# Branches around an expert's third token tile: behind every second weight tile instead of every fourth

## The chip, the cores and the metric

The kernel runs on one core of a Trainium2 chip. Its metric is the device time of one launch in microseconds (us). TensorE (PE in the profile; its weight loads are PEld) multiplies matrices, VectorE (DVE), ScalarE (ACT) and GpSimd (POOL) work on elements, and SyncE (SP) starts the transfers of weights from HBM into SBUF. Every engine runs its own list of instructions, and semaphores order them among each other.

## The reference

The reference is a decoder trunk of two layers over 256 tokens of width 1024. Each layer has a token mixer (three kinds of attention heads that share one projection) and a channel mixer, a SwiGLU: a dense one of width 2816 in layer 0, and in layer 1 a mixture of eight experts of width 3584. Only the experts matter here:

```python
def _swiglu(h, w_gate, w_up, w_down):
    return (jax.nn.silu(h @ w_gate) * (h @ w_up)) @ w_down

def _moe(h, router_w, w_gate, w_up, w_down):
    ...
    logits = (t @ router_w).astype(jnp.float32)
    top_val, top_idx = lax.top_k(logits, TOP_K)          # TOP_K = 2 of 8
    top_w = jax.nn.softmax(top_val, axis=-1)
    ...
    for e in range(N_EXPERTS):
        y = y + combine[:, e:e + 1] * _swiglu(t, w_gate[e], w_up[e], w_down[e])
```

Each token goes to two of eight experts, so an expert has 64 tokens on average. All weights are float32; the eight experts hold 8 x 3 x 1024 x 3584 x 4 bytes = 352 MB, which are read once.

## The kernel before

The kernel gathers an expert's tokens into at most 96 columns (`xg`, by a matmul with a one-hot matrix at line 1252), as three *token tiles* of 32. The weights are the moving side of the matmuls and the tokens the stationary side: four matmuls with 32 columns each stand beside each other on the array, one for each quarter of a weight tile's columns.

An expert's width of 3584 is cut into two halves of 2048 and 1536 (`WS`). For each half `moe_pass` runs `project` with the gate weights (PSUM `mm`), SiLU on ACT into `a`, `project` with the up weights (PSUM `up`), the product `a*up` on DVE (line 1337), and nine or twelve transposes (`turn_units`, line 1221) into `aT`. `back` multiplies `aT` with the down weights into `y`; it runs one half late, behind the next half's projections. When both halves are in `y`, `take` and `scatter` weight the result and add it to `X`.

A *weight tile* is one transfer of up to 1 MB into one of 14 buffers (`raw`): for gate and up one of eight blocks of 128 rows, for down two blocks of 128 rows. So a gate or up piece has eight weight tiles, the down piece of the first half eight and that of the second half six. SP starts the transfers in program order; each waits for its buffer to come free and for the transfer eight places earlier.

Expert 0 always runs all three token tiles. The other seven are sorted by load, and their counts stand in registers (`many`). For these, `project` and `back` run token tiles 0 and 1 plainly, and keep the third tile's matmuls for a branch: `third` emits an `If(many > 64)` whose body runs the third tile over the weight tiles collected so far. The first branch of a piece that starts a PSUM bank also has an else side that writes zeros (`zerb`, lines 1140 and 1141), since the bank would otherwise hold nothing. Where there is none, the else side holds one semaphore step that stands for the skipped matmuls. A scheduler decides where the two plain token tiles stand among the branches. Two conditions place the branches: line 1161 for gate and up, line 1186 for down.

Of the kernel before, what the change touches and what calls it, by code (L numbers as in the profile page):

```python
# [31 lines left out]
def kernel(  # L32
# [1087 lines left out]
    def pieces(src, r, n):  # L1120

        step = 2048 // n
        for i in range(0, r, step):
            m = min(step, r - i)
            yield i, m, load_w(src[:, i:i + m], m, n)

    def place(banks, t, w):

        per = 512 // w
        return banks[t // per], t % per * w  # L1130

    def third(many, run, b, o, n=None):

        with tc.If(many > 64) as more:
            run()
        if n != 0:
            with more.Else():
                for c in range(0, n, 256):
                    m = min(256, n - c)
                    pe.matmul(b[:, o + c:o + c + m], zerb, trib.rearrange("p a n -> p (a n)")[:, 0:m], start=(o + c == 0), stop=True,  # L1140
                              skip_group_check=True)

    def project(x, n, src, w, banks, many):

        nw = w // 4

        def tile_t(t, k, v):
            b, o = place(banks, t, nw)
            xs = x[:, k, C * n + 32 * t:C * n + 32 * t + 32]
            for j in range(4):  # L1150
                last_of = pe.matmul(b[32 * j:32 * j + 32, o:o + nw], xs, v[:, nw * j:nw * j + nw],  # L1151
                                    start=(k == 0 and o == 0), stop=(k == KD - 1), skip_group_check=True)
            return last_of.ins

        rows, z = [], nw
        for k0, m, raw in pieces(src, KD, w):
            for k in range(m):
                rows.append((k0 + k, raw[:, k]))
                for t in range(2 if many is not None else T3):
                    marks["x"] = tile_t(t, k0 + k, raw[:, k])  # L1160
            if many is not None and (k0 + m) % 4 == 0:
                third(many, lambda: [tile_t(2, k, v) for k, v in rows], *place(banks, 2, nw), n=z)
                rows, z = [], 0

    def back(aT, w, src, banks, first, last, many):

        nw = w // 4
        R = w // P

        def tile_t(t, m, v):  # L1170
            j, cc = m * P // nw, m * P % nw // P
            b, o = place(banks, t, 256)
            for q in range(4):
                last_of = pe.matmul(b[32 * q:32 * q + 32, o:o + 256], aT[:, cc, t, 32 * j:32 * j + 32], v[:, 256 * q:256 * q + 256],  # L1174
                                    start=(first and m == 0 and o == 0), stop=(last and m == R - 1), skip_group_check=True)
            return last_of.ins

        rows, z, tiles = [], 256 if first else 0, 0
        for ms, raw in down_tiles(src, w):
            for i, m in enumerate(ms):  # L1180
                v = raw[:, D * i:D * i + D]
                rows.append((m, v))
                for t in range(2 if many is not None else T3):
                    marks["y"] = tile_t(t, m, v)
            tiles += 1
            if many is not None and (tiles == 4 or ms[-1] == R - 1):
                third(many, lambda: [tile_t(2, m, v) for m, v in rows], *place(banks, 2, 256), n=z)
                rows, z, tiles = [], 0, 0

    def down_tiles(src, w):  # L1190


        if w // 4 % 256 == 0:
            v = src.rearrange("(g p i) n -> p g (i n)", p=P, i=2)
            for g in range(w // 256):
                yield [2 * g, 2 * g + 1], load_w(v[:, g:g + 1], 1, 2 * D)[:, 0]
        else:
            v = src.rearrange("(g p i) n -> p g (i n)", p=P, i=3)
            one = src.rearrange("(g p i) n -> p g i n", p=P, i=3)
            for g in range(w // 384):  # L1200
                yield [3 * g, 3 * g + 1], load_w(v[:, g:g + 1, 0:2 * D], 1, 2 * D)[:, 0]
                if g % 2:
                    yield [3 * g - 1, 3 * g + 2], load_w(one[:, g - 1:g + 1, 2], 2, D).rearrange("p a n -> p (a n)")
# [21 lines left out]
    def moe_pass(base):  # L1225
# [74 lines left out]
        def finish(p):  # L1300
            nonlocal ybanks
            e, aT, w, src, first, last = p
            if first:
                ybanks = [dn2_bank() for _ in range(2)]
            back(aT, w, src, ybanks, first, last, None if base or e == 0 else many[e])
            if last:
                late.append((e, turn_hot(e), *take(ybanks)))

        for e in range(NE):
# [12 lines left out]
            for s_, w in enumerate(WS):  # L1322
                nw = w // 4
                gs = groups(nw)
                gb = [mm_bank() for _ in gs]
                project(xg, (e + 1) % 2, wg[:, :, c0:c0 + w], w, gb, None if base or e == 0 else many[e])
                a = fpm.tile([P, T3, 512], F32, tag="a", name="a", bufs=1)
                for b, t0, n in gs:
                    act.activation(a[:, t0:t0 + n, 0:nw], gb[b][:, 0:n * nw].rearrange("p (t n) -> p t n", t=n), AF.Silu)  # L1329
                if late:  # L1330
                    with tc.issue_after(marks["x"]):
                        scatter(*late.pop())
                ub = [up_bank() for _ in gs]
                project(xg, (e + 1) % 2, wu[:, :, c0:c0 + w], w, ub, None if base or e == 0 else many[e])
                for b, t0, n in gs:
                    av = a[:, t0:t0 + n, 0:nw]
# [29 lines left out]
    many = [None]  # L1366
# [94 lines left out]
```

## Time and profile before

| what | us |
|---|---|
| three timed runs | 1403.47, 1404.56, 1405.38 (median 1404.56) |
| profiled execution | 1399.66 |
| its span, first to last instruction | 1397.8 |
| PE busy | 1328.8 (95%) |
| DVE, ACT, POOL busy | 515.0, 366.1, 226.9 |
| expert stage, from about 540 us on: weight stream | about 420 GB/s in most slices |

The span has two parts: attention and the dense layer up to about 540 us, and the experts after it. In the second part the transfer engines move about 420 GB/s nearly all the time, and PE is busy 9 tenths or more of nearly every slice. The page counts a matmul as busy until its modelled end; matmuls overlap, so that a run's busy time is a little longer than the distance to the next run's start. Each float32 matmul of the program stands twice in the trace.

### The profile page before, as it was taken

Reading aid. Unit: us, or ns where it says so; the run is one execution under the profiler, and the core shown is the slowest. Engines: PE = TensorE matmul, PEld = TensorE weight load, DVE = VectorE, ACT = ScalarE, POOL = GpSimd, SP = SyncE. Lnnn points to the kernel's source line nnn. Section 1 sums busy time; section 2 is a strip of 40 time slices with the busy share of each in tenths; the row PEclk is TensorE's granted clock in tenths of the full one; section 3 lists DMA queues with packets and bytes.
Section 4 is the critical chain, followed back from the end, with each engine's and each line's share of the span. In section 5 each row is a group of like instructions: output and inputs, shape, how many; then the busy total and the mean of one; then the engine's idle time right before and its main releaser. Section 6 shows DMA issues by size and latency. Waiting matters only on the chain. (4 is left out here: it accounts for less than half of the span.)

```text
span 1397.8 us, 29383 instructions
## 1 busy us (share of the span) xinstructions
PE 1328.8 (95%) x12537; PEld 770.6 (55%) x12537; DVE 515.0 (37%) x778; ACT 366.1 (26%) x750; POOL 226.9 (16%) x257
## 2 busy tenths in 40 slices
PE   7999989999999999999999999998999999999995
PEld 3767768889777774354553343452442453454542
DVE  5788687788895653000110200200200200210213
ACT  4476544444466741000100100100100100100102
POOL 3334345444552341000000000000000000000000
PEclk9999999999999999999999999999999999999997
DMA  9866567988773368999999999999999999999992
GB/s 356 338 225 214 207 229 267 325 295 308 264 266 111 118 249 298 297 423 416 403 422 421 419 422 422 418 422 421 420 422 422 416 423 422 382 420 408 418 420 94
DMA packets 104678, 476.85 MB, mean 341 GB/s; under 512 B 8220, under 2 KB 17060, under 8 KB 75854
## 3 DMA queue, kind: packets, MB, share of 16 engines
q1 hardware_dynamic: 104278, 473.77, 86.4%
q8 instruction: 116, 1.90, 0.5%
q10 hardware_dynamic: 152, 0.80, 0.1%
q14 instruction: 36, 0.29, 0.1%
q0 software_dynamic: 96, 0.08, 0.0%
HBM read 472.78 MB, written 1.84 MB: 340 GB/s over the span
## 5 line engine op out<-in xcount | busy, mean ns | idle before, releaser
L1174 PE MATMUL y<-raw,aT 128*32 128x256 f32 x4480 | 258.2, 380 | 12.5 <-DMA raw<-in_moe_w_down_dram 5.5
L1151 PE MATMUL up<-raw,xg 128*32 128x512 f32 (+1 forms) x2560 | 255.5, 540 | 3.8 <-DMA raw<-in_moe_w_up_dram 2.8
L1151 PE MATMUL mm<-raw,xg 128*32 128x512 f32 (+1 forms) x2560 | 250.9, 540 | 4.9 <-DMA raw<-in_moe_w_gate_dram 2.5
L1174 PEld LDWEIGHTS y<-raw,aT 128*32 128x32 f32 x4480 | 157.3, 110 | 110.0 <-issue 17.0
L1151 PEld LDWEIGHTS up<-raw,xg 128*32 128x32 f32 x2560 | 82.4, 110 | 160.8 <-issue 150.5
L136 POOL TENSOR_TENSOR lo<-raw,hi 128x192 fp32r<-128x192 f32 x126 | 145.7, 1161 | 150.9 <-ACT hi L130 140.2
L1151 PEld LDWEIGHTS mm<-raw,xg 128*32 128x32 f32 x2560 | 81.9, 110 | 158.5 <-issue 138.7
L1337 DVE TENSOR_TENSOR a<-a,up 128x512 f32<-128x512 f32 (+1 forms) x48 | 29.8, 621 | 364.2 <-PE up L1151 226.2
L134 DVE TENSOR_TENSOR lo<-raw,hi 128x832 fp32r<-128x832 f32 (+2 forms) x126 | 136.4, 1090 | 41.8 <-ACT hi L130 37.0
L130 ACT CAST hi<-raw 128x1024 fp32r<-128x1024 f32 (+2 forms) x126 | 124.8, 1001 | 102.7 <-PE mm L153 43.8
L1377 POOL TENSOR_SCALAR ss_f<-ss_f 128x1 f32<-128x1 f32 x2 | 0.4, 218 | 856.9 <-ACT up L1375 856.9
L152 PE MATMUL mm<-hi,xT_hi 128*128 128x512 f32 (+2 forms) x336 | 131.8, 395 | 0.0
L153 PE MATMUL mm<-hi,xT_lo 128*128 128x512 f32 (+2 forms) x336 | 130.8, 389 | 0.5 <-DVE xT_lo L366 0.5
L154 PE MATMUL mm<-lo,xT_hi 128*128 128x512 f32 (+2 forms) x336 | 129.8, 388 | 1.3 <-DVE lo L134 1.3
L282 DVE SCALAR_TENSOR_TENSOR acc<-raw,c_act,acc 128x1024 f32<-128x1024 f32 x80 | 108.6, 1357 | 6.0 <-DMA raw<-in_w_ada_dram 5.5
L1329 ACT ACTIVATE a<-mm 128x512 f32<-128x512 f32 (+1 forms) x48 | 26.1, 544 | 212.6 <-PE mm L1151 148.8
L1222 ACT COPY aT<-tp 128x512 f32<-128x512 f32 (+1 forms) x32 | 16.0, 506 | 248.4 <-PE tp L1221 248.2
L154 PEld LDWEIGHTS mm<-lo,xT_hi 128*128 128x128 f32 x336 | 64.6, 192 | 12.9 <-DVE lo L134 2.8
L1222 DVE COPY aT<-tp 128x512 f32<-128x512 f32 x16 | 11.1, 692 | 164.1 <-PE tp L1221 164.0
L152 PEld LDWEIGHTS mm<-hi,xT_hi 128*128 128x128 f32 x336 | 64.8, 193 | 11.7 <-ACT a L836 1.4
L153 PEld LDWEIGHTS mm<-hi,xT_lo 128*128 128x128 f32 x336 | 64.8, 193 | 11.4 <-DVE xT_lo L366 1.3
L1267 ACT COPY Y<-y 32x256 f32<-32x256 f32 x48 | 17.5, 366 | 198.5 <-DVE Y L1265 198.0
(363 smaller groups left out, 1344.3 us busy)
## 6 DMA issues: line engine op xcount, KB each, us to landing
raw<-in_moe_w_down_dram SPq DMA_DIRECT2D x112, 1024.0 KB
raw<-in_moe_w_gate_dram SPq DMA_DIRECT2D x64, 1024.0 KB
raw<-in_moe_w_up_dram SPq DMA_DIRECT2D x64, 1024.0 KB
raw<-in_moe_w_gate_dram SPq DMA_DIRECT2D x64, 768.0 KB
raw<-in_moe_w_up_dram SPq DMA_DIRECT2D x64, 768.0 KB
raw<-in_w_ada_dram SPq DMA_DIRECT2D x40, 1024.0 KB
raw<-in_w_in_dram SPq DMA_DIRECT2D x12, 1024.0 KB
raw<-in_ffn_w_down_dram SPq DMA_DIRECT2D x10, 1024.0 KB
```

The lines of the kernel that those rows point to most:

```text
L130: act.copy(hv, raw)
L134: marks["lo"] = dve.tensor_sub(lo[:, :n1], f[:, :n1], hi[:, :n1]).ins
L136: pool.tensor_sub(lo[:, n1:a * n], f[:, n1:], hi[:, n1:a * n])
L152: pe.matmul(ps, xh, wh, start=start, stop=False)
L153: pe.matmul(ps, xl, wh, start=False, stop=False)
L154: pe.matmul(ps, xh, wl, start=False, stop=stop)
L282: dve.scalar_tensor_tensor(acc, raw[:, j], ck, acc, op0=OP.mult, op1=OP.add)
L1151: last_of = pe.matmul(b[32 * j:32 * j + 32, o:o + nw], xs, v[:, nw * j:nw * j + nw], start=(k == 0 and o == 0), stop=(k == KD - 1), skip_g ...
L1174: last_of = pe.matmul(b[32 * q:32 * q + 32, o:o + 256], aT[:, cc, t, 32 * j:32 * j + 32], v[:, 256 * q:256 * q + 256], start=(first and m ...
L1222: (dve.tensor_copy if b0 == 4 else act.copy)(flat[:, b0 * P:(b0 + len(part)) * P], tb[:, :len(part) * P])
L1329: act.activation(a[:, t0:t0 + n, 0:nw], gb[b][:, 0:n * nw].rearrange("p (t n) -> p t n", t=n), AF.Silu)
L1337: dve.tensor_mul(av, av, ub[b][:, 0:n * nw].rearrange("p (t n) -> p t n", t=n))
```

## The change

Both conditions change: in `project` a branch is emitted behind every second weight tile, and in `back` too.

```diff
@@ project
-            if many is not None and (k0 + m) % 4 == 0:
+            if many is not None and (k0 + m) % 2 == 0:
                 third(many, lambda: [tile_t(2, k, v) for k, v in rows], *place(banks, 2, nw), n=z)
                 rows, z = [], 0
@@ back
-            if many is not None and (tiles == 4 or ms[-1] == R - 1):
+            if many is not None and (tiles == 2 or ms[-1] == R - 1):
                 third(many, lambda: [tile_t(2, m, v) for m, v in rows], *place(banks, 2, 256), n=z)
                 rows, z, tiles = [], 0, 0
```

On PE, in the first gate piece of the last expert, from its first matmul on. `mm` is the PSUM bank, `xg` the tokens, `raw` the weights; the rows at line 1151 between a COMPARE_AND_BRANCH and the next UNCONDITIONAL_BRANCH are the third token tile, the other rows at line 1151 tiles 0 and 1 (eight matmuls a weight tile). Before:

```order
L1151 MATMUL mm<-raw,xg 32x512 x24
L1134 COMPARE_AND_BRANCH
L1151 MATMUL mm<-raw,xg 32x512 x16
L1134 UNCONDITIONAL_BRANCH
L1140 LDWEIGHTS zerb
L1140 MATMUL mm<-trib,zerb 128x256
L1140 LDWEIGHTS zerb
L1140 MATMUL mm<-trib,zerb 128x256
L1134 UNCONDITIONAL_BRANCH
L1151 MATMUL mm<-raw,xg 32x512 x32
L1134 COMPARE_AND_BRANCH
L1151 MATMUL mm<-raw,xg 32x512 x16
```

The same piece now, from behind the zeros of its first branch to the bottom of the piece:

```order
L1151 MATMUL mm<-raw,xg 32x512 x16
L1134 COMPARE_AND_BRANCH
L1151 MATMUL mm<-raw,xg 32x512 x8
L1134 UNCONDITIONAL_BRANCH x2
L1151 MATMUL mm<-raw,xg 32x512 x16
L1134 COMPARE_AND_BRANCH
L1151 MATMUL mm<-raw,xg 32x512 x8
L1134 UNCONDITIONAL_BRANCH x2
L1151 MATMUL mm<-raw,xg 32x512 x16
L1134 COMPARE_AND_BRANCH
L1151 MATMUL mm<-raw,xg 32x512 x8
L1134 UNCONDITIONAL_BRANCH x2
```

One branch without zeros has become three, each over 8 matmuls instead of 16, and between two branches stand 16 plain matmuls instead of 32.

On PE, at the end of the last expert's last down piece (`y` is its PSUM, `aT` the turned products; 16 plain matmuls are one weight tile). Before:

```order
L1174 MATMUL y<-raw,aT 32x256 x32
L1134 COMPARE_AND_BRANCH
L1174 MATMUL y<-raw,aT 32x256 x32
L1134 UNCONDITIONAL_BRANCH x2
L1174 MATMUL y<-raw,aT 32x256 x32
L1134 COMPARE_AND_BRANCH
L1174 MATMUL y<-raw,aT 32x256 x16
L1134 UNCONDITIONAL_BRANCH x2
L1174 MATMUL y<-raw,aT 32x256 x16
```

Now:

```order
L1134 COMPARE_AND_BRANCH
L1174 MATMUL y<-raw,aT 32x256 x16
L1134 UNCONDITIONAL_BRANCH x2
L1174 MATMUL y<-raw,aT 32x256 x32
L1134 COMPARE_AND_BRANCH
L1174 MATMUL y<-raw,aT 32x256 x16
L1134 UNCONDITIONAL_BRANCH x2
L1174 MATMUL y<-raw,aT 32x256 x32
L1134 COMPARE_AND_BRANCH
L1174 MATMUL y<-raw,aT 32x256 x16
L1134 UNCONDITIONAL_BRANCH x2
L1174 MATMUL y<-raw,aT 32x256 x16
```

Two branches have become three; the longest skip, over 32 matmuls, is gone, and the last plain weight tile still stands behind the last branch.

## Rows read from the trace of the kernel before

**Rows 1.** The page's costliest groups: form and count | busy, mean ns | idle before.

```profile
L1174 PE MATMUL y<-raw,aT 128*32 128x256 f32 x4480 | 258.2, 380 | 12.5 <-DMA raw<-in_moe_w_down_dram 5.5
```

**Rows 2.** One line's instructions, line 1140: count, ns min/median/max, first and last start.

```profile
L1140 PE MATMUL y<-trib,zerb x4: 283/283/283, 720.0 to 1350.8; 128*128 128x256 bf16 x4
```

**Rows 3.** Timeline of PE, straight runs: start, us, form, count [idle before].

```profile
616.16 20.93 PE L1174 MATMUL y<-raw,aT 128*32 128x256 f32 x384
...
1175.01 20.81 PE L1151 MATMUL up<-raw,xg 128*32 128x512 f32 x192
1195.63 0.61 PE L1174 MATMUL y<-raw,aT 128*32 128x256 f32 x8
...
1250.87 20.95 PE L1174 MATMUL y<-raw,aT 128*32 128x256 f32 x384
```

**Rows 4.** Stages: window, length, busy PE, PEld, DVE, ACT, POOL; PEclk, DMA, GB/s.

```profile
937.00:1046.00 109.00, 102.33 (x1238) 45.18 (x1234) 14.26 (x24) 10.77 (x23) 0.00 (x0) 1.00 1.01 421
1046.00:1153.00 107.00, 106.05 (x1338) 46.41 (x1331) 11.75 (x20) 8.13 (x17) 0.00 (x0) 1.00 1.01 420
1153.00:1273.00 120.00, 119.90 (x1511) 56.24 (x1509) 13.18 (x24) 10.09 (x22) 0.00 (x0) 1.00 1.00 409
1273.00:1376.00 103.00, 99.50 (x1283) 47.65 (x1286) 13.95 (x24) 9.89 (x23) 0.00 (x0) 1.00 0.93 384
```

**Rows 5.** Waits of PE, 940 to 1046 us: us in total, times, longest.

```profile
PE y L1174 <- DMA raw<-in_moe_w_down_dram: 3.0, 4, 1.3
PE up L1151 <- DMA raw<-in_moe_w_up_dram: 2.4, 4, 1.0
```

**Rows 6.** Waits of PE, 1046 to 1376 us.

```profile
PE y L1174 <- issue: 1.9, 1, 1.9
...
PE mm L1151 <- DMA raw<-in_moe_w_gate_dram: 0.5, 1, 0.5
```

**Rows 7.** Stages, the end of the weight stream.

```profile
1370.00:1376.00 6.00, 5.65 (x104) 3.53 (x100) 0.83 (x2) 0.21 (x1) 0.00 (x0) 1.00 0.08 30
```

**Rows 8.** Timeline of PE in the last expert.

```profile
1293.84 7.07 PE L1151 MATMUL up<-raw,xg 128*32 128x512 f32 x64
1301.09 1.92 PE L1151 MATMUL up<-raw,xg 128*32 128x512 f32 x16 [0.18 <-PEq L1134]
...
1367.18 3.66 PE L1174 MATMUL y<-raw,aT 128*32 128x256 f32 x64
1371.02 3.66 PE L1174 MATMUL y<-raw,aT 128*32 128x256 f32 x64 [0.18 <-PEq L1134]
1374.85 1.93 PE L1174 MATMUL y<-raw,aT 128*32 128x256 f32 x32 [0.17 <-PEq L1134]
```

**Rows 9.** One line's instructions, the branch line 1134.

```profile
L1134 PEldq COMPARE_BRANCH  x120: 70/179/2089, 640.9 to 1373.2; - x120
L1134 PEldq EVENT_SEMAPHORE  x28: 51/51/51, 641.7 to 1374.7; - x28
```

**Rows 10.** Timeline of PE, its last waits for weights.

```profile
979.70 5.60 PE L1174 MATMUL y<-raw,aT 128*32 128x256 f32 x100 [0.49 <-DMA raw<-in_moe_w_down_dram]
...
1035.72 4.42 PE L1174 MATMUL y<-raw,aT 128*32 128x256 f32 x64 [1.29 <-DMA raw<-in_moe_w_down_dram]
...
1045.66 10.51 PE L1151 MATMUL mm<-raw,xg 128*32 128x512 f32 x96 [0.54 <-DMA raw<-in_moe_w_gate_dram]
```

**Rows 11.** Waits of SP's queue from 560 us on.

```profile
SPq L113 <- DMA raw<-in_moe_w_down_dram: 141.0, 73, 2.7
```

**Rows 12.** Timeline of PE, two long idle times at skips.

```profile
1094.06 1.93 PE L1174 MATMUL y<-raw,aT 128*32 128x256 f32 x32 [0.77 <-PEq L1134]
...
1359.05 0.59 PE L1174 MATMUL y<-raw,aT 128*32 128x256 f32 x3
1361.57 1.92 PE L1174 MATMUL y<-raw,aT 128*32 128x256 f32 x29 [1.93 <-issue]
```

## The prediction

> **What bounds the kernel now.** I read the table of stages first, then TensorE's waits on either side of one moment (1046 us), then the branch line itself, then single runs of matmuls.
>
> An expert with at most 64 tokens skips its third token tile; I call it light, the others heavy. Counting matmuls, 4480 at line 1174 [rows 1] are twice 2240 (the trace shows every fp32 matmul twice): expert 0 has 336, seven others 224 each, which leaves 336 for third tiles, at 112 each three experts. So three are heavy and four light, and four `zerb` matmuls on `y`, the last at 1350.8 us, say the same [rows 2]. That last one puts a light expert at the end. Of the order in time: a run of 192 up matmuls without a break [rows 3] marks a heavy expert, `zerb` matmuls a light one, and so the eight are: expert 0 (no branch), light, light, heavy, light, heavy, heavy, light.
>
> In the table of stages the reader is to see that both resources look full [rows 4]: weights at 409 to 421 GB/s and TensorE busy for 102.33 of 109 us before 1046 us, 119.90 of 120 in the second of the two neighbouring heavy experts. Busy shares can't choose between them; waits can. From 940 to 1046 us TensorE waits eight times for down and up weights (3.0 and 2.4 us) [rows 5]. From 1046 to 1376 us the only weight wait is the one with which that window opens, 0.5 us; the longest of the rest is "issue", 1.9 us, TensorE's own sequencer [rows 6]. So up to 1046 us the weight stream sets the time, and from there to 1376 us TensorE does, without slack, with one stretch of light work (the fifth expert's last down piece, at 1086 to 1096 us) and the last light expert inside. At the end the weights have run out (30 GB/s after 1370 us [rows 7]) while TensorE still works to 1376.8 us [rows 8].
>
> **The change part by part.** *More branches.* Per expert: 2 become 4 in two gate pieces, two up pieces and the first down piece, and 2 become 3 in the second down piece (six weight tiles): 12 to 23, 84 to 161 in all. Five of them also write zeros where the tile is skipped; those stay five. A light expert thus passes 18 plain skips instead of 7.
>
> *What a plain skip costs on TensorE.* The arm's else side is an EVENT_SEMAPHORE, 28 in the trace [rows 9], seven for each of four light experts. It waits for TensorE's own earlier matmuls, so the pipeline runs empty and fills again. Price: 64 up matmuls with one skip behind them take 1301.09 - 1293.84 = 7.25 us [rows 8]; 192 without a break take 1195.63 - 1175.01 = 20.62, so 64 take 6.87 [rows 3]. Difference 0.38. In the down piece 64 take 3.84 (1367.18 to 1371.02) and 3.83 us [rows 8] against 64/384 of 20.93 = 3.49 [rows 3]: 0.35. I take 0.37. Only half of it shows as idle time (0.18 [rows 8]); the other half is the overlap of neighbouring matmuls that is lost. The low end is therefore 0.18, the high end 0.38.
>
> The Trainium skill (Advanced Engine Details and Errata, Control Flow Timing) gives about 51 ns for a plain branch and about 108 ns for a compare-and-branch. The trace has 51 ns for the semaphore step, but 70 to 2089 ns for the compare. By the page's prices alone 12 skips would cost an estimated 1.9 us and the kernel would come out at 1406.5 us; the rows say 0.35 to 0.38 a skip, because the drain, not the instruction, is paid.
>
> *Where it counts.* After 1046 us: 11 more skips in the last expert, and one more in the fifth expert's last down piece. 12 x 0.37 = 4.4 us on the path, bounds 2.2 and 4.6. Queued behind a waiting semaphore step are the next weight tiles' matmuls, and for these wait ACT and DVE (`a`, `Y`) and, at the end, the whole tail; nothing absorbs the delay. The granted clock is 1.00 (the 2.4 GHz level) in light and heavy stretches alike [rows 4], so the clock stays out of the sum.
>
> *Skips before 1046 us.* 33 less that one, 32, cost 12 us of TensorE time, but the stream sets the time there. The tightest place is the fifth expert: between the waits that end at 979.70 and 1035.72 us six more skips (two gate, two up, two down) come to 2.2 us, against idle times of 1.29 and 0.54 us that they use up [rows 10]. 0.4 us is left. It is paid back right there: at 1045.66 us TensorE waits for the third weight tile of a heavy expert while third-token-tile work on the first two could run; behind four tiles it may not, behind two it may. I cost this at 0, bounds -0.5 and +0.4. If the cover were gone (a stream that runs earlier), up to 2.2 us would show.
>
> *Executed arms.* In the heavy experts the arm falls through. 384 down matmuls take 20.93 us in expert 0, which has no branch, and 20.95 in a heavy expert with two [rows 3]: 0.01 us a branch. 22 more after 1046 us cost 0.2 us. The cover is the queue of matmuls that TensorE's sequencer has issued ahead; without it, the compare (median 179 ns [rows 9]) would stand bare, 22 x 0.18 = 4.0 us. The number of matmuls is the same on both sides, so nothing else is added.
>
> *Weight buffers and other queues.* A buffer is free after two tiles' arm instead of four, so transfers may be issued earlier. After 1046 us TensorE waits for no transfer, so this buys nothing. SP passes 77 more block borders, but stands mostly in waits for earlier transfers (141.0 us for down weights alone [rows 11]); ACT and DVE are busy 10.09 and 13.18 us of 120 [rows 4]. All three at 0; if an SP issue came late it would have to be by more than the stream's lead to reach TensorE.
>
> **Sum**, on the profiled execution (1399.66 us, span 1397.8): 4.4 + 0.2 + 0 = 4.6 us, 1404.3 us. The timed runs of before have a median of 1404.56, 4.9 us above the profiled one; the difference is carried over: 1409.2 us. Own range of this case: 2.2 - 0.5 = 1.7 to 4.6 + 0.2 + 0.4 = 5.2 us more, 1406.3 to 1409.8 us; I stand near its top because the skips measured at 0.35 to 0.38 are the nearest rows.
>
> **Rivals.** (1) *Skips that wait for code.* One compare took 2089 ns [rows 9] (the idle time at 1094.06 us is 0.77 instead of 0.18, 0.6 more), and 0.2 us after a skip, inside a plain run of matmuls, TensorE stood 1.93 us for nothing that the profile shows [rows 12]: 2.5 us over the 14 skips after 1046 us, those with zeros included, 0.18 for each. If each taken branch carries that risk, 12 more add 2.2 us: 1411.4 us. For it: both stalls lie at skips, and a drained queue leaves a stall bare. Against: the skipped distance is the same in sum, in shorter steps. The Trainium skill (Runtime: NRT & Kernel Launch, Instruction fetch mechanics) says that a taken branch whose target lies outside the fetched window makes the engine wait for a fetch. The two stalls agree with it; that jumps are the cause no run here shows yet.
>
> (2) *Stalls that go.* One of the two stalls came right behind a skip over 32 matmuls of the program, the other at the next skip after one of 32; no skip is longer than 16 now. If neither comes back, 2.5 us are gained: 4.6 - 2.5 = 2.1 more, 1406.7 us, no difference that can be told. That also covers skips that cost only the idle 0.18 us (2.4 more). For it: the stalls are few and single. Against: the code still has to be fetched.
>
> (3) *Faster: the stream gets its lost time back.* From 1153 to 1273 us the stream ran at 409 instead of 421 GB/s [rows 4], 120 x 12/421 = 3.4 us, since buffers stood in arms of four tiles. Freed by twos it would run full, and if the end were set by the last weight's landing, the kernel would take 1401.2 us. It decides if TensorE stands waiting for weights in the last 100 us; [rows 6] show no such wait, and TensorE still works when the stream has ended [rows 7, 8]. Little speaks for it.
>
> (4) *It doesn't do what it says*: if the scheduler put the new branches side by side, a second drain would find the pipeline already empty. The order has 16 or more matmuls between them in the last expert, so I give this no chance of its own.
>
> **How the numbers follow.** The forecast has 0.60, rival 1 0.15, rival 2 0.20, rival 3 0.05. The predicted time is that of the forecast, 1409.2 us. 0.2% is 2.8 us, about what a measurement of this kernel tells from no change: slower means above 1407.4, faster below 1401.8. The forecast's own range lies above 1407.4 but for about a twentieth of its chance (0.03); with rival 1 slower gets 0.72, rival 2 and that rest make 0.23 for the same, rival 3 gives 0.05. The range goes down to 1405.3 (stalls gone and skips priced midway between their bounds, 12 x 0.25 + 0.2 - 2.5 = 0.7 us more) and up to 1412.0 (rival 1 with 0.6 us of bare compares in the heavy experts).
>
> **What would show it.** In the profile of the changed kernel line 1134 has 72 EVENT_SEMAPHORE instead of 28 and 161 + 69 = 230 COMPARE_BRANCH instead of 120. In the last expert runs of 64 matmuls become runs of 32, each followed by 0.18 us idle for the branch line. 384 down matmuls of a heavy expert stay at 20.9 to 21.2 us. The weights still end near 1372 us, and the last run of down matmuls starts at about 1379.4 instead of 1374.85 us. I am wrong if TensorE waits for weights after 1100 us, if such a run has no idle time behind it, or if "issue" stalls of 2 us come in a number other than one or two.

## The result, and the profile after

The changed kernel takes 1413.51 us (median of six runs, 1409.63 to 1415.83) against 1405.38 us in six runs of before beside it: ratio 1.0057, 95% interval 1.0038 to 1.0075, so 5.3 to 10.5 us slower, 8.1 in the middle. Forecast were 4.6 us, at most 7.4. A repeat beside later versions gave 1.0058 (1.0040 to 1.0077). The sign was right, the size too small.

Runs of one kernel scatter by up to 13 us, mostly with TensorE's mean granted clock, which each run lists (0.977 to 0.988): a straight line through all timed runs, with a level of its own for each kernel, falls by 0.89 us per 0.001 of clock and leaves a scatter of 1.4 us. Differences *at equal clock* below are levels of that fit. There the change costs 7.2 and 7.3 us (each ±1.1). The twelve runs of the changed kernel have a mean clock of 0.981, those of before 0.982; if the change itself lowers it, the fit leaves that part out.

First what the forecast had said of the branch line and of the last expert. The branch line 1134 after, which answers to [rows 9] (count, ns min/median/max, first and last start):

```profile
L1134 PEldq COMPARE_BRANCH  x230: 70/176/3128, 644.9 to 1386.1; - x115
L1134 PEldq EVENT_SEMAPHORE  x72: 51/51/51, 645.7 to 1387.7; - x72
```

TensorE's timeline after, in the last expert and in the heavy expert before it (answers to [rows 3, 8, 12]; start, us, form, count [idle before]):

```profile
1258.46 22.28 PE L1174 MATMUL y<-raw,aT 128*32 128x256 f32 x384
...
1284.24 3.64 PE L1151 MATMUL mm<-raw,xg 128*32 128x512 f32 x32
1288.07 3.64 PE L1151 MATMUL mm<-raw,xg 128*32 128x512 f32 x32 [0.18 <-PEq L1134]
1291.88 3.64 PE L1151 MATMUL mm<-raw,xg 128*32 128x512 f32 x32 [0.17 <-PEq L1134]
...
1369.60 3.66 PE L1174 MATMUL y<-raw,aT 128*32 128x256 f32 x64 [1.81 <-PEq L1134]
...
1383.95 3.66 PE L1174 MATMUL y<-raw,aT 128*32 128x256 f32 x64 [0.17 <-PEq L1134]
1387.78 1.93 PE L1174 MATMUL y<-raw,aT 128*32 128x256 f32 x32 [0.17 <-PEq L1134]
```

72 and 230 are the predicted counts. Each skip has its 0.17 to 0.18 us: gate matmuls come in runs of 32 (the down piece's last weight tiles had breaks at this distance before, too). Start to start such a run takes 3.81 us, where 32 of an unbroken run take 20.62/6 = 3.44 [rows 3]: 0.37 a skip, as priced. The last run of down matmuls starts at 1387.78 instead of 1374.85 us; 4.0 us of that stand already at the first transposes of the expert stage (583.12 against 579.09 us), ahead of any branch.

TensorE's waits after, 1046 to 1390 us, which answer to [rows 6] (us in total, times, longest):

```profile
PE y L1174 <- PEq L1134: 3.0, 8, 1.8
PE mm L1151 <- PEq L1134: 1.0, 6, 0.2
PE up L1151 <- PEq L1134: 0.9, 5, 0.2
PE y L1174 <- issue: 0.2, 1, 0.2
```

No wait for a transfer is left: TensorE still sets the time to the end, and but for the longest, 1.8 us, and the "issue" of 0.2 all of it is skips of 0.17 to 0.2 us. The stages, though, hold two things that were not forecast (window, length, busy PE, PEld, DVE, ACT, POOL; PEclk, DMA, GB/s):

```profile
1255.00:1260.00 5.00, 5.00 (x45) 4.13 (x45) 0.92 (x3) 0.64 (x2) 0.00 (x0) 0.78 1.01 421
1260.00:1265.00 5.00, 5.00 (x88) 2.70 (x86) 0.00 (x0) 0.00 (x0) 0.00 (x0) 0.88 0.93 362
...
1370.00:1376.00 6.00, 5.59 (x95) 3.22 (x84) 0.00 (x0) 0.00 (x0) 0.00 (x0) 1.00 0.82 332
1376.00:1382.00 6.00, 5.75 (x81) 3.73 (x83) 0.69 (x1) 1.20 (x3) 0.00 (x0) 1.00 0.07 26
```

The granted clock was 0.78 and 0.88 there: a part of these 10 us ran at the lower level, 1.2 GHz, while TensorE was busy without a break before and behind; the 384 down matmuls above took 22.28 instead of 20.95 us. The repeat has no such stretch at this place, but one in the last expert, at once behind its longest idle time (granted clock 0.72 from 1370 to 1376 us); 64 down matmuls take 5.35 instead of 3.66 us there:

```profile
1370.43 5.35 PE L1174 MATMUL y<-raw,aT 128*32 128x256 f32 x64 [2.03 <-PEq L1134]
```

```profile
1370.00:1376.00 6.00, 5.40 (x68) 3.34 (x72) 0.00 (x0) 0.00 (x0) 0.00 (x0) 0.72 0.88 358
```

And the weights end near 1377 us, not 1372. Of these 5 us or a little more, too, 4.0 are the later start of the stage; the rest is a stream that runs about 2 us late. Where does it become late? In the first expert with branches (the second in time). TensorE's timeline there, before:

```profile
641.79 12.65 PE L1151 MATMUL mm<-raw,xg 128*32 128x512 f32 x115 [0.22 <-PEq L1134]
...
656.20 12.65 PE L1151 MATMUL up<-raw,xg 128*32 128x512 f32 x115
...
692.34 7.94 PE L1151 MATMUL mm<-raw,xg 128*32 128x384 f32 x94 [0.19 <-PEq L1134]
```

and after:

```profile
646.67 12.65 PE L1151 MATMUL mm<-raw,xg 128*32 128x512 f32 x115 [1.06 <-PEq L1134]
...
661.91 12.65 PE L1151 MATMUL up<-raw,xg 128*32 128x512 f32 x115 [0.98 <-PEq L1134]
...
697.80 0.85 PE L1151 MATMUL mm<-raw,xg 128*32 128x384 f32 x8 [0.58 <-PEq L1134]
```

Here the scheduler puts all branches of a gate or up piece side by side, after the piece's first matmuls and ahead of 115 plain ones. Three skips in a row cost 1.06 us, one cost 0.22. From 592 to 692 us TensorE waits for no transfer in either profile, so this lies on the path: a buffer comes free when TensorE has passed it.

A table sums this up. The first transposes of each half (line 1221) mark the time on TensorE; these are the distances between such marks in us, from the repeat of before (whose marks start at 583.08, as those of after do at 583.12, and which took 1404.5 us where the first profiled execution took 1399.66):

| stretch | before | before again | after | after again |
|---|---|---|---|---|
| A: expert 0's second half, first branching expert's first half | 105.91 | 106.14 | 107.60 | 107.55 |
| B: to the fifth expert (940 us) | 255.48 | 255.85 | 255.70 | 255.71 |
| C: to the last expert (1272 us) | 331.27 | 331.39 | 334.25 | 332.18 |
| D: last expert, first gate and up piece | 46.73 | 46.73 | 48.41 | 48.48 |
| E: first down, second gate and up piece | 44.94 | 45.05 | 47.07 | 48.29 |
| F: to the start of the last down matmul | 12.98 | 12.98 | 13.19 | 13.19 |
| G: from there to the end | 21.40 | 21.42 | 21.82 | 22.06 |

The sum of the differences between after and before again is 8.48 us; the two executions lie 8.42 apart. A gives 1.46, C 2.86 (about 1.6 of it the stretch at half clock), D to F 3.91, G 0.40. In the repeat of after D to F give 5.20, of which about 1.7 are its stretch at half clock, and C only 0.79.

C holds a loss that shows no idle time. In each of the three heavy experts the second gate piece takes 0.57 us longer, with the same 192 matmuls. In the last heavy expert, before again and after again:

```profile
1217.62 15.69 PE L1151 MATMUL mm<-raw,xg 128*32 128x384 f32 x192
```

```profile
1221.64 16.26 PE L1151 MATMUL mm<-raw,xg 128*32 128x384 f32 x192
```

Four matmuls that stand beside each other start together, one such group every 0.33 us, 48 groups in all. In the changed kernel the trace has 50 starts: at 1222.31 and 1222.63 us one matmul starts alone, and later two groups have three. The scheduler has put the branch inside a group of four, and the single matmul takes a group's time; it does so twice, since each float32 matmul stands twice. The second gate piece of the last expert has the same split: it takes 12.62 us against 11.26 in before again, the up piece behind it 11.86 against 11.10. Both have two skips more; the 0.60 between them is the split group. Every version with gate and up by two or by one in these experts has it, no other.

### The profile page after: what moved, and what is told of

Its sections match the earlier page's. It is cut to its first block, busy times and chain, and to the rows that moved or that the text cites. A ratio compares the mean times of both kernels' runs of the same rounds, so it can differ in the third digit from the quotient of the medians.

```text
span 1411.2 us, 29582 instructions
## 1 busy us (share of the span) xinstructions
PE 1337.4 (95%) x12537; PEld 785.3 (56%) x12537; DVE 514.7 (36%) x778; ACT 365.8 (26%) x750; POOL 225.5 (16%) x257
## 5 line engine op out<-in xcount | busy, mean ns | idle before, releaser
L1151 PE MATMUL mm<-raw,xg 128*32 128x512 f32 (+1 forms) x2560 | 256.0, 541 | 6.3 <-PEq L1134 4.9
L1151 PEld LDWEIGHTS mm<-raw,xg 128*32 128x32 f32 x2560 | 90.2, 110 | 156.7 <-issue 117.0
L1151 PEld LDWEIGHTS up<-raw,xg 128*32 128x32 f32 x2560 | 85.4, 110 | 161.4 <-issue 147.2
```

## The experiments

In all versions the two conditions take a parameter, and a table gives each expert (1 to 7 in order of time, 7 the last) its distance between branches, 4 where it names none:

```diff
-            if many is not None and (k0 + m) % 4 == 0:
+            if many is not None and (k0 + m) % step == 0:
...
-            if many is not None and (tiles == 4 or ms[-1] == R - 1):
+            if many is not None and (tiles == step or ms[-1] == R - 1):
```

Below, `P_STEP` is the table for gate and up, `B_STEP` that for down. The marks of the versions (stretches as above), and the difference at equal clock (±0.8 for twelve runs, ±1.0 for eight, ±1.1 for six):

| version | A | C | D | E | F | timed |
|---|---|---|---|---|---|---|
| before again | 106.14 | 331.39 | 46.73 | 45.05 | 12.98 | 0 |
| first by 2 | 107.57 | 333.52 | 46.74 | 44.11 | 12.98 | +1.4 |
| last by 2 | 106.11 | 333.78 | 48.24 | 46.13 | 13.20 | +2.2 |
| all but first by 2 | 105.97 | 332.42 | 48.25 | 45.60 | 13.19 | +2.7 |
| heavy by 2 | 105.94 | 332.39 | 46.74 | 42.33 | 14.37 | -1.1 |
| last by 1 | 106.10 | 331.59 | 52.89 | 51.70 | 14.97 | +16.1 |
| first by 1 | 111.14 | 331.55 | 46.73 | 42.62 | 15.22 | +6.9 |
| gate and up by 2 | 107.53 | 332.75 | 48.24 | 43.89 | 13.66 | +4.4 |
| down by 2 | 106.14 | 332.74 | 46.74 | 43.32 | 13.19 | -3.0 |
| down by 2, again | 106.13 | 331.56 | 46.73 | 42.58 | 13.81 | -1.6 |
| down by 2, not the last | 105.96 | 331.07 | 46.73 | 43.51 | 13.30 | -1.8 |
| last by 8 | 106.12 | 331.05 | 45.96 | 48.16 | 13.68 | +0.2 |
| light by 8 | 105.57 | 333.12 | 45.96 | 44.61 | 15.24 | +1.6 |
| mixture | 105.54 | 331.56 | 45.96 | 48.86 | 12.60 | +0.9 |
| before, 12 transposes more | 106.07 | 331.64 | 46.73 | 44.08 | 12.98 | -1.0 |
| before, 24 transposes more | 105.92 | 331.80 | 46.73 | 43.78 | 14.07 | -1.0 |
| after, 24 transposes more | 107.62 | 332.85 | 48.48 | 46.12 | 13.18 | +5.9 |

**The parts of the change, by expert.** Theory A is the forecast's skip price plus the first expert's side-by-side skips; B a price for any branch anywhere; C puts the loss on the heavy experts' arms and buffers.

```diff
+    P_STEP, B_STEP = {1: 2}, {1: 2}
```

> Branches behind every second weight tile in the first branching expert alone (the second in order, light); all others every fourth. Theory A (a plain skip costs TensorE a drain, and it counts where TensorE sets the time; in this expert the added branches stand side by side in the gate and up pieces and hold TensorE while the weight stream waits for its buffers): +2.4 us, as the stream's landings moved in the changed kernel (from +4.0 to +6.4 us between 640 and 700 us). Theory B (each branch costs the same wherever it stands: 8 us over 77 branches, 0.10 us each): 11 more branches, +1.1 us. Theory C (the loss comes from the heavy experts, whose arms and buffers changed): 0.

Measured: 1405.71 us, ratio 0.9999 (0.9979 to 1.0019), 1.4 us slower at equal clock. A shows 1.43 us more, as the whole change has there (1.41 and 1.46). The total lies below theory A's 2.4.

```diff
+    P_STEP, B_STEP = {7: 2}, {7: 2}
```

> Every second weight tile in the last expert alone (light). Theory A: 11 more plain skips at 0.37 us, all on the path: +4.1 us, in runs of 32 matmuls with 0.18 us idle behind each. Theory B: 11 x 0.10 = +1.1 us. Theory C: 0.

Measured: 1409.01 us, 1.0013 (0.9996 to 1.0029). D is 1.51 us longer for four more skips, 0.38 each. The whole, 2.2 at equal clock, is less than theory A's 4.1: E grew by 1.08 us only, with six skips and a split group more, since its idle time is shorter than in before again (1.73 against 0.25 and 1.93 us) and no down matmuls start in twos behind it.

```diff
+    P_STEP, B_STEP = {e: 2 for e in range(2, 8)}, {e: 2 for e in range(2, 8)}
```

> Every second weight tile in all branching experts but the first. Theory A: the whole change without the first expert's 2.4 us: 8.1 - 2.4 = +5.7 us by the timed medians, +4.6 us by my sum. Theory B: 66 x 0.10 = +6.9 us. Theory C: the whole +8 us. The weight stream's landings after 700 us should not move against before (theory A); with B and C they move as in the changed kernel.

Measured: 1409.14 us, 1.0022 (1.0008 to 1.0037); D and F behave as in the last version, E is 0.5 us shorter. At equal clock 2.7 us, less than theory A's 4.6 to 5.7 and far from B's 6.9 and C's 8.

```diff
+    P_STEP, B_STEP = {e: 2 for e in (3, 5, 6)}, {e: 2 for e in (3, 5, 6)}
```

> Every second weight tile in the three heavy experts alone (third, fifth and sixth of the branching ones). Theory A: executed arms cost 0.01 us a branch, 33 more branches, +0.3 us: no difference. Theory B: 33 x 0.10 = +3.4 us. Theory C: the most of the +8 us.

Measured: 1404.97 us, 0.9989 (0.9974 to 1.0005). The whole is no slower than before (interval -3.7 to +0.7 us, where B had +3.4 and C most of 8): B and C fall. Inside, the split groups cost their 0.57 us in each heavy expert (16.26 us three times), and E, without a branch changed, is 2.7 us shorter since its long idle time is gone.

**Both places made larger.** A branch behind every tile, in the last or in the first branching expert:

```diff
+    P_STEP, B_STEP = {7: 1}, {7: 1}
```

> Only the last expert changes: a branch behind every weight tile (41 plain skips instead of 7), the seven others as before. Theory A (each plain skip costs 0.37 us where TensorE sets the time): 34 x 0.37 = 12.6 us more, interval to hold +12.6; runs of 32 plain matmuls (one weight tile) each with about 0.18 us idle for the branch line. Theory D (each taken skip also carries the risk of a code stall, 0.18 us on average, as rival 1 of the prediction had it): 34 x 0.55 = 18.7 us more, and several stalls of 1 to 3 us in the last expert. Theory B (0.10 us for any branch): 3.4 us more.

Measured: 1420.67 us, 1.0121 (1.0100 to 1.0141), so 14.1 to 19.8 us more. TensorE's timeline at the head of its first gate piece:

```profile
1277.39 1.91 PE L1152 MATMUL mm<-raw,xg 128*32 128x512 f32 x10
1279.22 0.39 PE L1141 MATMUL mm<-trib,zerb 128*128 128x256 bf16 x2
1279.55 1.06 PE L1152 MATMUL mm<-raw,xg 128*32 128x512 f32 x6
1280.77 1.92 PE L1152 MATMUL mm<-raw,xg 128*32 128x512 f32 x16 [0.17 <-PEq L1135]
1282.87 1.92 PE L1152 MATMUL mm<-raw,xg 128*32 128x512 f32 x16 [0.17 <-PEq L1135]
```

A run of 16 takes 2.10 us start to start, 1.72 unbroken (20.62 x 16/192): 0.38 a skip again, at half the distance. Theory A's 12.6 us were short by 3.5. The first branch splits a group of four here, too: the 10 and 6 matmuls in the first and third row are one weight tile, four groups, but they start as 4, 4, 1 and 1, and behind the zeros as 3 and 3, six starts some 0.43 us apart. That is 0.86 us in a piece of 512 columns; D holds two such pieces, and grew by 6.16 us = 12 x 0.37 + 2 x 0.86; E has three split groups more than before, at 0.6 each (34 starts for 32 in the gate piece, 38 for 34 in the up piece). Together 3.5 us. Single stalls have no share in that: no idle time over 0.7 us shows in the last expert.

```diff
+    P_STEP, B_STEP = {1: 1}, {1: 1}
```

> Only the first expert with branches changes: a branch behind every weight tile, the other six as before. There gate and up branches stand side by side on TensorE, and TensorE, not the stream, sets the time from 592 to 692 us. Theory A' (the stream takes TensorE's delay there over and keeps it to the end): in every second tile's version the weight landings came 2.4 us later; with three times as many extra skips (34 instead of 11, of which about two thirds before 692 us) 5 to 7 us more in the total, and the landings of the last expert's weights later by as much. Theory E (the stream makes it good again within the following experts, as the time of the version with every second tile in this expert alone, +0.3 us, would have it): within 1.5 us of before, the landings of the last expert's weights where they were.

Measured: 1412.35 us, 1.0063 (1.0043 to 1.0083). TensorE's timeline where the branches stand side by side:

```profile
646.51 12.65 PE L1152 MATMUL mm<-raw,xg 128*32 128x512 f32 x115 [2.84 <-PEq L1135]
...
663.50 12.65 PE L1152 MATMUL up<-raw,xg 128*32 128x512 f32 x115 [2.74 <-PEq L1135]
...
701.08 1.02 PE L1152 MATMUL mm<-raw,xg 128*32 128x384 f32 x8 [2.28 <-PEq L1135]
```

Seven skips, 2.84 us: 0.41 each. One light expert of seven now costs about as much as the whole change. The stages behind it, before, after, and in this version (columns as above), show what becomes of it:

```profile
692.00:740.00 48.00, 45.56 (x557) 23.08 (x560) 5.18 (x8) 2.26 (x5) 0.00 (x0) 1.00 1.00 412
```

```profile
692.00:740.00 48.00, 43.69 (x541) 21.91 (x544) 8.54 (x14) 6.07 (x14) 0.00 (x0) 1.00 0.99 395
```

```profile
692.00:740.00 48.00, 41.77 (x481) 19.41 (x482) 9.45 (x17) 6.33 (x14) 0.00 (x0) 1.00 0.93 369
```

412, 395, 369 GB/s: buffers come free later and the stream stands. From 640 to 740 us SP's queue waits 20.2 us for the branch line, 4.2 in before again. From 740 to 1046 us the stream runs at 420 or 421 GB/s in all three and can't make it up. At the fifth expert (A and B together) TensorE is 6.35 us later than in before again. E falls, A' holds (5 to 7 forecast, 6.9 at equal clock).

**By kind of piece.**

```diff
+    P_STEP, B_STEP = {e: 2 for e in range(1, 8)}, {}
```

> Every second weight tile in the gate and up pieces of all seven experts, the down pieces as before. Theory A: 8 more plain skips in the last expert x 0.37 = 3.0 us, and the side-by-side skips of the first branching expert add up to 2.4 us: 3.0 to 5.4 us more. Theory D adds 8 x 0.18 = 1.4. Theory C (the down arms of heavy experts carry the loss): within 1.5 us of before.

```diff
+    P_STEP, B_STEP = {}, {e: 2 for e in range(1, 8)}
```

> Every second weight tile in the down pieces of all seven experts, the gate and up pieces as before. Theory A: 3 more plain skips in the last expert and one in the fifth expert's last down piece x 0.36 = 1.4 us more; no side-by-side skips. Theory C (down arms and the freeing of down buffers): most of the 8 us.

Measured: 1408.98 us, 1.0027 (1.0013 to 1.0041), within theory A; and 1401.88 us, 0.9977 (0.9959 to 0.9994): *faster* than before by 3.2 us, where A had 1.4 slower. A fails there as a whole; C falls once more.

**The other way, a mixture, and the change again.**

```diff
+    P_STEP, B_STEP = {7: 8}, {7: 8}
```

> Only the last expert changes, the other way: one branch for a whole piece (every eighth weight tile), so 1 plain skip there instead of 7. Theory A (a plain skip costs 0.37 us where TensorE sets the time): 6 x 0.37 = 2.2 us less than before. Theory F (the third tile's arm at the end of a piece holds eight of the fourteen weight buffers until it is passed, and the weights come late): no gain, or up to 3 us slower, with TensorE waiting for weights in the last 100 us.

Measured: 1405.79 us, 1.0005 (0.9990 to 1.0019). D is 0.77 us shorter for two skips fewer: A's price holds below, too. But the down piece loses more than that. Its timeline:

```profile
1353.55 1.93 PE L1175 MATMUL y<-raw,aT 128*32 128x256 f32 x32 [0.50 <-DMA raw<-in_moe_w_down_dram]
1356.04 1.93 PE L1175 MATMUL y<-raw,aT 128*32 128x256 f32 x32 [0.55 <-DMA raw<-in_moe_w_down_dram]
1358.52 1.93 PE L1175 MATMUL y<-raw,aT 128*32 128x256 f32 x32 [0.55 <-DMA raw<-in_moe_w_down_dram]
1360.39 0.28 PE L1141 MATMUL y<-trib,zerb 128*128 128x256 bf16 x1
1361.13 1.05 PE L1175 MATMUL y<-raw,aT 128*32 128x256 f32 x10 [0.46 <-DMA raw<-in_moe_w_down_dram]
1365.11 2.78 PE L1175 MATMUL y<-raw,aT 128*32 128x256 f32 x22 [2.93 <-issue]
```

Buffers held by eight tiles make the weights late (theory F, 2.1 us in four waits), and behind the long skip TensorE stands 2.93 us that the profile gives no releaser for. The granted clock falls there (0.52 from 1364 to 1368 us), and the 22 matmuls take 2.78 us.

```diff
+    P_STEP, B_STEP = {e: 8 for e in (1, 2, 4, 7)}, {e: 8 for e in (1, 2, 4, 7)}
```

> One branch for a whole piece in the four light experts, the heavy ones as before. Theory A: the 2.2 us of the last expert, and what the first branching expert's skips (0.22 us idle twice) hold the stream up, 0 to 0.6: 2.2 to 2.8 us less than before. Theory F: in the light experts in the middle the stream sets the time, and buffers held for eight tiles make it stop: 1 to 5 us slower than with the last expert alone.

Measured: 1408.96 us, 1.0032 (1.0017 to 1.0048): the time is the one of F, and B is 2.4 us longer than in before again. But F's mechanism does not show in the middle experts: from 740 to 940 us the stream runs at 421 GB/s as before, and from 685 to 945 us TensorE waits 6.1 us for weights against 5.9 in before again. What grew there are idle times without data (5.8 us in two against 3.3 in four), and the granted clock falls behind them (0.50 from 732 to 736 us).

```diff
+    P_STEP = {1: 8, 7: 8}
+    B_STEP = {**{e: 2 for e in range(1, 7)}, 7: 8}
```

> Where plain skips lie on TensorE's path, fewer of them (one branch a piece in the last expert, and in the gate and up pieces of the first branching expert), and in the down pieces of the six other experts a branch behind every second tile. Theory A, from the skips alone: 6 fewer in the last expert, one more in the fifth expert's last down piece: -2.2 + 0.4 = -1.8 us, to -2.4 with the first expert. Theory G (the gain of 3.2 us that the down pieces alone showed is one of the down arms, beside the cost of their four more skips on the path): -3.2 - 1.1 - 2.2 = -6.5 us.

Measured: 1404.35 us, 1.0006 (0.9989 to 1.0023): neither theory. Its first down piece of the last expert waits for weights as above, and then:

```profile
1362.85 0.40 PE L1141 MATMUL y<-trib,zerb 128*128 128x256 bf16 x1 [4.61 <-issue]
```

The changed kernel, without an edit:

> The whole change once more, beside the versions above. Theory A: 11 more skips in the last expert and one in the fifth (4.4), and the first branching expert's side-by-side skips (2.4): +6.8 us. If the effects of gate and up (+3.8) and of down (-3.2) simply added: +0.6.

Measured: 1414.45 us, 1.0058 (1.0040 to 1.0077). The parts do not add: the first branching expert alone (+1.4) and all the others (+2.7) make 4.1 of 7.3 at equal clock, gate and up with down 1.4.

**Idle times that follow no data.** Four runs ask whether these hang on the instructions' place in the program. The padded versions put small transposes ahead of the third expert's second half, where TensorE waits for weights:

```diff
+            for _ in range(PAD if b0 == 0 and len(turned) == 5 else 0):
+                pe.transpose(tb[:8, 0:8], ident[:8, :8], ident[:8, :8])
             for i, (cc, t) in enumerate(part):
```

> The kernel before, word for word, profiled once more. If the idle times without data hang on the program: again one of about 1.9 us 0.2 us into the matmuls behind the first skip of the last expert's last down... (at 1361.57 us in the profile of before), and 0.77 us at 1094. If they hang on chance: other places or lengths.

Measured: 1404.5 us (one run). Idle times at the same places, 1.93 us again, and 0.89 where 0.77 was; TensorE's timeline at the longer one, which answers to [rows 12]:

```profile
1360.06 4.39 PE L1174 MATMUL y<-raw,aT 128*32 128x256 f32 x63 [0.25 <-issue]
1366.38 1.92 PE L1174 MATMUL y<-raw,aT 128*32 128x256 f32 x29 [1.93 <-issue]
```

1.93 us, 29 matmuls ahead of the piece's end, as in the first profile. In this program, then, they repeat.

With 12 transposes:

> The kernel before with 12 small transposes (8x8) ahead of the third expert's second half, at about 777 us, where TensorE waits for weights (5.3 us of such waits from 690 to 940 us). They shift all later TensorE instructions in the program by 12 transposes and add nothing else. Theory P (the idle times hang on the position in the program): the one at 1361.57 us moves, shrinks or grows by 1 us or more, and the time moves by as much, 0 to 2 us either way. Theory Q (they hang on the branches' number and distance): the same idle times at the same places, time within 0.5 us.

Measured: 1405.88 us, 1.0000 (0.9982 to 1.0018). The idle time stands at the skip itself now, 2.13 us, and the one of 0.77 has 1.07.

With 24:

> As the version with 12, with 24 such transposes. Theory P: other idle times again, time 0 to 2.5 us off either way. Theory Q: as before.

Measured: 1404.80 us, 0.9994 (0.9977 to 1.0010): 1.56 us at the skip, and one of 0.53 at another place. Both versions are 1.0 us (±0.8) faster at equal clock: E is 1.0 and 1.3 us shorter, though in the second F is 1.1 us longer.

The changed kernel with 24:

> The changed kernel with 24 such transposes at the same place. Theory P: the idle time of 1.8 us behind the skip at 1366 us (2.0 in its repeat) moves or changes by 1 us or more; the time +5 to +9 us against before. Theory Q: the same 1.8 to 2.0 us, +7.3 to +8.9 us.

Measured: 1410.48 us, 1.0041 (1.0024 to 1.0059), 5.9 us at equal clock: 1.71 us at the same skip. So neither theory is whole: a shift of the instructions moves these idle times and changes them by tenths of a microsecond, and the time by about 1 us.

**Down pieces alone, again, and without the last expert's.**

> Every second weight tile in the down pieces of all seven experts, once more. If the gain is the version's: 2 to 4 us less than before again. If it was scatter: within 1.5 us of before.

Measured: 1401.55 us, 0.9965 (0.9946 to 0.9984). The gain repeats. Its first down piece of the last expert has two skips more than before, and this timeline:

```profile
1356.62 3.66 PE L1175 MATMUL y<-raw,aT 128*32 128x256 f32 x64
1360.46 3.66 PE L1175 MATMUL y<-raw,aT 128*32 128x256 f32 x64 [0.18 <-PEq L1135]
1364.30 3.66 PE L1175 MATMUL y<-raw,aT 128*32 128x256 f32 x64 [0.17 <-PEq L1135]
1368.25 1.93 PE L1175 MATMUL y<-raw,aT 128*32 128x256 f32 x32 [0.29 <-PEq L1135]
```

No long idle time is left, and the matmuls run evenly. E has 42.58 us against 45.05, with 0.7 us of skips added. The first execution of the same program had one at this place, so an idle time need not repeat:

```profile
1362.80 1.93 PE L1175 MATMUL y<-raw,aT 128*32 128x256 f32 x32 [1.02 <-PEq L1135]
```

```diff
+    P_STEP, B_STEP = {}, {e: 2 for e in range(1, 7)}
```

> Every second weight tile in the down pieces of six experts, the last one as before. Theory A: only the fifth expert's one more skip counts, +0.4 us; against the version with all down pieces 1.1 us less. If that version's gain is real, 4 us less than before.

Measured: 1401.80 us, 0.9976 (0.9958 to 0.9995): as fast, not faster. The version with every down piece by two is the best of the study: 3 to 5 us faster than before by the ratios, 1.6 to 3.0 at equal clock, where the whole change is 7.3 us slower.

**What ends the long idle times.** The traces hold the transfers of instructions, too. The page of before has them as a queue of its own:

```profile
q8 instruction: 116, 1.90, 0.5%
```

These are blocks of 16 KB, in the expert stage one every 8.8 us on average, each about 1 us long. In the twenty traces TensorE has 52 idle times of 0.7 us or more in the experts that no weight transfer and no other engine ends, if those at the side-by-side skips of the first branching expert are left out. All 52 end 2.2 to 2.7 us after such a block began, and 1.2 to 1.7 us after its last byte; a moment picked at random would do so one time in twenty. In before, the block of the 1.93 us began at 1358.99 and ended at 1360.10 us, and TensorE went on at 1361.57. The 14 idle times at side-by-side skips (0.98 to 2.84 us) are of another kind: they grow with the number of skips. So the long idle times are waits for code, as far as times can show it; the page does not say which engine a block is for. That skips and padding place them by shifting when TensorE comes to its next block is the nearest reading, but no run shows it by itself.

## Why the prediction was too small

*Price of a skip in the last expert: right; the sum there near by luck.* 11 x 0.37 = 4.07 us were forecast. D alone, which has no long idle time in any profile, gives 0.38 a skip for two fewer and four more, and 0.37 for twelve more when the split groups are taken off. D to F grew by 3.91 us (after against before again), by 5.20 in the repeat of after (3.5 without its stretch at half clock) and by 3.02 in the padded version. But these hold a split group of 0.6 us that was not forecast. By the difference, 0.8 to 1.2 us of E were gained against before again, where the down matmuls behind the idle times start in twos at several places (68 starts for 64 groups; 66 and 64 after). The two nearly cancel.

*"Skips before 1046 us" at 0: wrong, and this is the first step that failed.* The prediction said that the stream sets the time up to 1046 us and looked for the tightest place in the fifth expert. It had read TensorE's waits from 940 us on only. In the first branching expert TensorE waits for no weight, and what it loses there the stream loses, too, since its buffers come free later. Stretch A grew by 1.4 to 1.5 us in every version that branches there by two. At the fifth expert (A and B together) TensorE was 1.3 us late in both executions of after, 1.1 in its padded version and 2.0 with the first expert alone, where the versions with this expert's gate and up pieces by four stand between 0.8 us early and 0.3 late. A stage that is bound by the stream passes a delay on; it hides only what TensorE makes good before the buffer is needed.

*"The number of matmuls is the same on both sides, so nothing else is added": wrong, and this is the second step that failed.* The arms themselves are as cheap as forecast: 384 down matmuls of a heavy expert take 20.95 us in the repeat of after as before [rows 3]. But the order of the matmuls changed. Where the first branch of a gate piece splits a group of four, the piece takes 0.57 us longer; after 1046 us this happens in two heavy experts and in the last one, 1.7 us that the sum had at nothing. Together with the first branching expert that is 2.8 to 3.0 us, about what the forecast fell short by at equal clock (7.3 - 4.6 = 2.7).

*"Side by side" as a rival without a chance: wrong.* It was dismissed since the branches of the last expert stand apart; in the first branching expert they do stand side by side. And its mechanism was wrong as well: a second drain does not find the pipeline already empty and cheap. Seven skips in a row take 0.41 us each.

*The Trainium skill's prices* (Advanced Engine Details and Errata, Control Flow Timing) would have had 1406.5 us with 51 ns for a branch and 108 ns for a compare-and-branch; the trace has 0.37 to 0.41 us a skip on TensorE.

*Rivals 1 and 2.* Rival 1 had the mechanism that the long idle times point to, waits for code, but not the price: 34 more skips in the last expert brought no more of them (1.7 us in three pieces, against 1.93 in one), so there is no fixed risk per taken branch. Rival 2 came half true: in the fifth expert's last down piece the idle time of 0.77 us (0.89 in before again) has gone, with 0.17 at that skip in both executions of after, and the other one stayed, 1.8 to 2.0 us. *Rival 3* fell: no wait for weights is left to gain from.

*What stays open.* By the marks, with the stretches at half clock left out, the change costs 6.2 to 6.9 us: 1.3 up to the fifth expert; in C 0.8 to 1.2 (one skip 0.4, two split groups 1.1, less the 0.7 of the idle time that went); 3.5 to 3.9 in D to F; 0.4 to 0.6 in the tail G, and why that is longer was not tried. The prediction's place for the end of the weights, 1372 us, fails by the same late stream. That the parts measured alone make only 4.1 is explained in part by E: the version without the first expert has one idle time of 0.44 us there, the whole change one of 1.8 to 2.0. The Trainium skill's rule on taken branches that leave the fetched window (Runtime: NRT & Kernel Launch, Instruction fetch mechanics) fits the 52 idle times that end behind a block of instructions; that the jump of a skip is what asks for the block is not shown by itself. It is not shown either why the same program has an idle time of 1.02 us in one execution and 0.29 in another, why even a padded version of before gains 1 us, and what makes the down pieces by two faster.

## What to carry to other kernels

Price a skipped branch on a busy engine by the rows around an existing one (run with a skip minus run without), and multiply only after the waits of *every* stretch that holds such branches have been read; a stretch without transfer waits lies on the path even if the stages behind it are bound by the stream. Look at the order of instructions at each place, not at one: a scheduler may put branches apart in one expert and side by side in another, and may put one inside a group of matmuls that would run beside each other. The count of matmuls does not show that; the length of the same run in both profiles does (15.69 against 16.26 us). Effects of a few tenths of a per cent that come from where instructions stand make parts not add; a version that is padded without other change shows how large they are.

## What the runs showed of the hardware

A skipped arm costs TensorE 0.37 to 0.38 us between runs of matmuls whether these have 16, 32 or 64, and 0.41 us in a chain of skips; an executed arm costs 0.01. A matmul of 32 columns that is split off from its group of four takes the time of the whole group: 0.57 us for a float32 matmul of 384 columns in a heavy expert, 0.86 with 512 in the last expert by 1. Idle times of 0.4 to 4.6 us without any data dependence stand behind skips; the longest (2.93, 3.67, 4.61) came in the three versions whose skip spans a whole piece, and all of 0.7 us or more end 1.2 to 1.7 us behind a 16 KB block of instructions. Single short stretches at 1.2 GHz (granted clock 0.78 and 0.88 in two windows of 5 us, 0.72 in one of 6) come in the expert stage in some executions, in others of the same kernel not; they cost about 1.6 us each where TensorE sets the time (a heavy expert's half took 62.65 us instead of 61.04 in the repeat). Some follow an idle time of about 2 us or more, others come in a run of matmuls without a break.
